# Three sums of weight quarters queued at the priority of their splits, and the scalar gates' columns moved behind the first mixer's projections

## The chip, the cores and the metric

The kernel runs on one core of a Trainium2 chip. The metric is the device time of one execution in microseconds (us), as a median of several runs. Five engines matter here: TensorE (PE in the profile; PEld is its weight load), VectorE (DVE), ScalarE (ACT), GpSimd (POOL) and SyncE (SP), which issues the transfers. Each works through its own list of instructions in the order in which they stand, and waits at the head of the list when an operand is not there.

## What is computed

A decoder trunk of two layers on 512 tokens of 1024 features, in float32:

```python
for i in range(DEPTH):                       # DEPTH = 2
    x = x + 0.5 * swiglu_ffn(rmsnorm(x, ffn1_norm[i]), ffn1_w_gu[i], ffn1_w_down[i])
    xn = rmsnorm(x, mix_norm[i])
    x = x + (ab_mixer(xn, ...) if i % 2 == 0 else nsa_mixer(xn, ...))
    x = x + 0.5 * swiglu_ffn(rmsnorm(x, ffn2_norm[i]), ffn2_w_gu[i], ffn2_w_down[i])
return rmsnorm(x, final_norm)
```

`swiglu_ffn` is `(silu(x @ w_gate) * (x @ w_up)) @ w_down` with 2816 hidden features. `ab_mixer` projects `xn` once into 512 channels of a gated linear recurrence (RG-LRU) and four mLSTM heads, whose scalar input and forget gates are eight columns of the projection. `nsa_mixer` is a sparse attention.

## The kernel before

**Products.** Every float32 operand is split in two: `hi`, its rounded part (ACT, a copy into float32r), and `lo`, the rest (DVE or POOL, `raw - hi`). A product of 128x128 weights is three matmuls, `hi*hi`, `hi*lo`, `lo*hi` (`mm3`, lines 177 to 179); the third is the first that needs the weights' `lo`. Weights stream from HBM: a transfer into a raw buffer (SP), the `hi` copy (ACT, line 171 or 320), the `lo` difference (line 172 or 321), then PE.

**The feed-forward blocks** (four, named f0a, f0b, f1a, f1b here). Of 22 slices of 128 hidden features the first four are multiplied directly; each of the other 18 is a pair (gate and up weights) that runs as seven products of half width after Strassen and Winograd, p1 to p7, each of twelve 256-column matmuls. They come in groups of 4, 8 and 6 slices; after each group the down projection of the group is added. `Pair.load` (line 301) brings a pair's four weight quarters (four transfers, lines 307 to 310, into two tiles `ra` and `rc`, both called `r` in the profile), forms three sums of them on DVE (lines 311 to 313; the first makes two sums at once) and splits the seven operands in four steps of `hi` (line 320) and `lo` (line 321): `ra[0:2]` for p1 and p7, `rc[0:2]` for p2 and p6, `ra[2:4]` for p5 and p4, and half as large `rc[2:3]` for p3. Two pairs of `r` tiles take turns, so that the transfers of a pair wait until the last splits of the pair two before have read their tile.

PE's order is written out by hand: p1, p7, then p3 of the pair before, p6, p2, p4, p5. The evictions of the products (lines 338 to 370) and what follows p3, the product of gate and up (line 372, DVE) and its `hi` and `lo` (line 390, ACT, and 391, DVE), are left to the scheduler like the sums and splits. The order of all engines but PE comes out of it: an instruction inside `tc.high_priority(offset=n)` is asked for n places earlier than it is written. The transfers and the sums have offset 400 (`RAHEAD`; 180, `RFIRST`, for the first two pairs of a block), the splits 230 (`SAHEAD`; 110, `SFIRST`), the evictions 320 (`EV`).

**The first mixer** (`ab`, line 479). Four turns of a loop each make four projections (24 matmuls of 512 columns each): channels of the recurrence (`rg_conv`), q, k (`qk`), and the output gate (`out_gate`). In the first turn the scalar gates' projection is made too, and `gate_rows` (line 569) works out from it on DVE and ACT the rows `G` and `EM` (names `misc` in the profile), by 12 DVE and 3 ACT steps. `gate_cols` (line 586) transposes them with eight small PE matmuls (lines 590 and 591) and copies the 128x32 result on DVE (line 592); the columns `gcol` are first read in the mLSTM loop. It stands at the end of the second turn. Behind the loop come `rg_gate(3)`, `rg_scan` (the recurrence, four channel groups of six DVE steps and one on ACT) and `proj_tok` (the v projection, lines 228 to 230), then the mLSTM loop over four chunks (lines 648 to 685).

A short chain of 128x4 steps (`sp`, lines 505 to 519: a transfer of `lam`, then one ACT exponential between some 25 DVE steps) prepares a constant of the recurrence. It is written at the head of `ab`, and the scheduler places it inside the last group of f0a, since nothing but `lam`, which takes the place of an `r` tile, holds it back.

Of the kernel before, what the change touches and what calls it, by code (L numbers as in the profile page):

```python
# [24 lines left out]
SAHEAD = 230  # L25
RAHEAD = 400
SFIRST = 110
# [29 lines left out]
def build(tc, a, out, stages=("f0a", "ab", "f0b", "f1a", "nsa", "f1b")):  # L57
    nc = tc.nc
    with ExitStack() as ctx:
# [16 lines left out]
        def blk(i, dt, name):  # L76
            return bp.tile([P, BW.get(i, 4 * T)], dt, name=name, tag=f"b{i}")
# [11 lines left out]
        def psum2():  # L89
            return pp.tile([P, T], F32, name="pt", bufs=8 - PSB)  # L90
# [205 lines left out]
        class Pair:  # L296
# [4 lines left out]
            def load(self, w, rb, first=False):  # L301
                with tc.high_priority(offset=RFIRST if first else RAHEAD):
                    ra, rc = (blk(rb[2 * (turns[1] % 2) + i], F32, f"r{i}")[:, :4 * T]
                              .rearrange("p (s c) -> p s c", s=4) for i in range(2))
                    turns[1] += 1

                    nc.sync.dma_start(ra[:, 0], w[0][:, :T])
                    nc.sync.dma_start(rc[:, 3], w[1][:, :T])
                    nc.sync.dma_start(ra[:, 3], w[1][:, T:])
                    nc.sync.dma_start(rc[:, 0], w[0][:, T:])  # L310
                    nc.vector.tensor_add(ra[:, 1:3], ra[:, 0:4:3], rc[:, 3:4].to_broadcast([P, 2, T]))  # L311
                    nc.vector.tensor_add(rc[:, 1], ra[:, 0], ra[:, 2])
                    nc.vector.tensor_add(rc[:, 2], rc[:, 0], rc[:, 1])
                with tc.high_priority(offset=SFIRST if first else SAHEAD):
                    for src, names in ((ra[:, 0:2], ("B11", "Q7")), (rc[:, 0:2], ("B21", "Q6")),
                                       (ra[:, 2:4], ("Q5", "Q4")), (rc[:, 2:3], ("B22",))):
                        hi, lo = parts()
                        m = len(names) * T
                        src = src.rearrange("p s c -> p (s c)")
                        nc.scalar.activation(hi[:, :m], src, AF.Copy)  # L320
                        nc.vector.tensor_sub(lo[:, :m], src, hi[:, :m].bitcast(F32))  # L321
                        for n, name in enumerate(names):
                            self.W[name] = hi[:, n * T:(n + 1) * T], lo[:, n * T:(n + 1) * T]
                return self
# [152 lines left out]
        def ab(x, nxt):  # L477
# [108 lines left out]
            def gate_cols():  # L586
                ps = psum2()
                for c in range(NT):
                    cs = slice(c * P, (c + 1) * P)
                    nc.tensor.transpose(ps[:, c * 8:c * 8 + 4], G[:, cs], ident[:4, :4])  # L590
                    nc.tensor.transpose(ps[:, c * 8 + 4:c * 8 + 8], EM[:, cs], ident[:4, :4])
                nc.vector.tensor_copy(gcol, ps[:, :NT * 8])
# [27 lines left out]
            for i in range(4):  # L620
                rg_conv(i)
                if i == 0:
                    gate_in()
                qk(i)
                qk(4 + i)
                if i == 0:
                    gate_rows()
                else:
                    rg_gate(i - 1)
                out_gate(i)  # L630
                if i == 1:
                    gate_cols()
            rg_gate(3)

            rg_scan()
            pss = proj_tok(a["ab_v"], x)
# [523 lines left out]
        first = [w[1:] for w in w0] if stages[0] == "f0a" else None  # L1160
# [129 lines left out]
```

## Time and profile before

| what | value |
|---|---|
| median of 3 runs | 2067.31 us (2062.09 to 2072.84) |
| the profiled execution, its own time | 2052.11 us |
| its span | 2050.4 us, 30519 instructions |
| PE busy | 1976.9 us, 96% of the span |
| DVE, ACT, POOL busy | 1372.1, 1027.8, 280.1 us |

The profiled execution is one run of its own; it is 15.2 us below the median of the three timed runs. Its rows are read for differences. In the rows a name such as `DVE L321 ... wx<-r,wx` is an engine, a line of the kernel and what is written from what; `wx` and `whi`, `wlo` are places of the splits, `ps` and `pt` are PSUM tiles. A time in brackets is how long the engine stood idle before the instruction, and what ended that. SPq marks an issue of a transfer.

### The profile page before, as it was taken

What the parts mean: (1) busy time and instruction counts of PE and PEld (TensorE: products, weight loads), DVE (VectorE), ACT (ScalarE), POOL (GpSimd) and SP (SyncE); (2) the same over time, 40 slices, a digit from 0 to 9 for tenths busy, and PEclk for the clock granted to TensorE, in tenths of its full rate; (3) what the DMA queues carried; (4) which work ended last, traced back from release to release, by engine and by line L of the source; (5) the groups of instructions that cost most, each with busy time, mean ns of one, the idle gap of its engine ahead of it and who ended that gap; (6) DMA issues with size and microseconds to landing.
All of it is one profiled execution on the core that took longest, in us unless ns stands there. A gap on an engine that the chain in (4) does not pass through costs nothing.

```text
span 2050.4 us, 30519 instructions
## 1 busy us (share of the span) xinstructions
PE 1976.9 (96%) x11896; PEld 1729.3 (84%) x11896; DVE 1372.1 (67%) x2189; ACT 1027.8 (50%) x1900; POOL 280.1 (14%) x290
## 2 busy tenths in 40 slices
PE   8899899989999998999999999999999999999997
PEld 6889899867788998897889989877777678999896
DVE  7847657489758657475966847443778788658474
ACT  5525436355545445254534525433888855446252
POOL 3000000343120000002000000201655540000002
PEclk9999999999999999999999999999999999999998
DMA  5232322322222323232232333321001032323212
GB/s 186 84 102 83 114 83 76 99 73 84 91 93 89 117 90 108 76 111 91 93 113 93 106 93 106 112 83 62 25 23 31 23 108 79 117 83 114 87 63 88
DMA packets 74737, 182.10 MB, mean 89 GB/s; under 512 B 8416, under 2 KB 9184, under 8 KB 74592
## 3 DMA queue, kind: packets, MB, share of 16 engines
q1 hardware_dynamic: 74448, 180.06, 28.2%
q8 instruction: 93, 1.52, 0.3%
q14 instruction: 52, 0.43, 0.1%
q10 hardware_dynamic: 144, 0.09, 0.0%
HBM read 178.02 MB, written 2.10 MB: 88 GB/s over the span
## 4 chain that ended last, share of the span: by engine, by line
PE 60%; DVE 9%; DMA 4%; issue 4%; ACT 2%; POOL 1%; SPq 0%; POOLq 0%; DVEq 0%; ACTq 0%
PE ps L177 14%; PE ps L178 14%; PE ps L179 14%; DMA r<-wgu 3%; PE pt L177 3%; PE pt L179 3%; PE pt L178 3%; PE px L999 2%; PE pt L789 2%; PE pt L1016 1%; DVE wlo L321 1%; PE pt L1017 1%; DVE wlo L172 1%; PE ps L955 1%; PE ps L958 1%
## 5 line engine op out<-in xcount | busy, mean ns | idle before, releaser
L171 ACT ACTIVATE whi<-raw 128x1024 fp32r<-128x1024 f32 (+2 forms) x196 | 193.3, 988 | 361.7 <-PE ps L178 250.8
L178 PE MATMUL ps<-h,whi 128*128 128x512 f32 x704 | 276.1, 392 | 1.1 <-DVE h L391 1.1
L179 PE MATMUL ps<-h,wlo 128*128 128x512 f32 x704 | 276.6, 393 | 0.0
L177 PE MATMUL ps<-h,whi 128*128 128x512 f32 x704 | 274.8, 391 | 1.3 <-ACT h L390 1.3
L320 ACT ACTIVATE whi<-r 128x1024 fp32r<-128x1024 f32 (+1 forms) x174 | 165.6, 952 | 194.4 <-PE ps L178 151.7
L172 DVE TENSOR_TENSOR wlo<-raw,whi 128x1024 fp32r<-128x1024 f32 (+2 forms) x166 | 192.7, 1164 | 73.1 <-ACT whi L171 68.0
L118 POOL TENSOR_TENSOR acc<-acc,t 128x512 f32<-128x512 f32 x48 | 75.5, 1573 | 1124.9 <-ACT t L116 1119.8
L458 DVE SCALAR_TENSOR_TENSOR X<-ps,X 128x512 f32<-128x512 f32 x96 | 66.3, 691 | 229.0 <-PE ps L179 229.0
L321 DVE TENSOR_TENSOR wlo<-r,whi 128x1024 fp32r<-128x1024 f32 (+1 forms) x174 | 188.6, 1086 | 24.1 <-ACT whi L320 23.8
L177 PE MATMUL ps<-x,whi 128*128 128x512 f32 x432 | 179.2, 415 | 0.5 <-ACT x L106 0.5
L179 PE MATMUL ps<-x,wlo 128*128 128x512 f32 x432 | 171.5, 397 | 0.0
L178 PE MATMUL ps<-x,whi 128*128 128x512 f32 x432 | 171.1, 396 | 0.3 <-DVE x L107 0.3
L311 DVE TENSOR_TENSOR r<-r,r 128x1024 f32<-128x1024 f32 x72 | 88.1, 1224 | 122.9 <-DMA r<-wgu 122.5
L178 PEld LDWEIGHTS ps<-h,whi 128*128 128x128 f32 x704 | 132.3, 188 | 31.9 <-DVE h L391 2.6
L177 PEld LDWEIGHTS ps<-h,whi 128*128 128x128 f32 x704 | 132.3, 188 | 30.5 <-ACT h L390 2.1
L179 PEld LDWEIGHTS ps<-h,wlo 128*128 128x128 f32 x704 | 132.4, 188 | 27.7
L177 PE MATMUL ps<-qB,whi 128*128 128x256 f32 x520 | 145.5, 280 | 2.5 <-ACT ps L364 2.4
L179 PE MATMUL ps<-qB,wlo 128*128 128x256 f32 x520 | 144.9, 279 | 0.6 <-DVE wlo L321 0.6
L178 PE MATMUL ps<-qB,whi 128*128 128x256 f32 x520 | 145.0, 279 | 0.0
L321 DVE TENSOR_TENSOR wx<-r,wx 128x1024 fp32r<-128x1024 f32 (+1 forms) x114 | 123.3, 1083 | 22.7 <-ACT wx L320 20.9
L390 ACT ACTIVATE h<-t 128x512 fp32r<-128x512 f32 x88 | 55.4, 630 | 139.0 <-DVE t L372 136.5
L320 ACT ACTIVATE wx<-r 128x1024 fp32r<-128x1024 f32 (+1 forms) x114 | 107.2, 941 | 6.2 <-DVE r L311 4.1
(340 smaller groups left out, 5442.4 us busy)
## 6 DMA issues: line engine op xcount, KB each, us to landing
r<-wgu SPq DMA_DIRECT2D x288, 256.0 KB, 3.6
raw<-wd SPq DMA_DIRECT2D x64, 512.0 KB, 3.5
raw<-wgu SPq DMA_DIRECT2D x30, 512.0 KB, 3.5
raw<-wd SPq DMA_DIRECT2D x32, 384.0 KB, 3.1
raw<-ab_fm SPq DMA_DIRECT2D x21, 512.0 KB, 3.5
raw<-nsa_fm SPq DMA_DIRECT2D x17, 512.0 KB, 3.5
raw<-ab_out SPq DMA_DIRECT2D x8, 512.0 KB, 3.5
raw<-nsa_out SPq DMA_DIRECT2D x16, 256.0 KB, 2.6
```

Source lines behind the costliest of these rows:

```text
L118: nc.gpsimd.tensor_add(acc, acc, sq)
L171: nc.scalar.activation(hi[:, :n], raw[:, :n], AF.Copy)
L172: (eng or nc.vector).tensor_sub(lo[:, :n], raw[:, :n], hi[:, :n].bitcast(F32))
L177: nc.tensor.matmul(ps, wh, xh, start=start, stop=False, skip_group_check=on)
L178: nc.tensor.matmul(ps, wh, xl, start=False, stop=False, skip_group_check=on)
L179: nc.tensor.matmul(ps, wl, xh, start=False, stop=stop, skip_group_check=on)
L311: nc.vector.tensor_add(ra[:, 1:3], ra[:, 0:4:3], rc[:, 3:4].to_broadcast([P, 2, T]))
L320: nc.scalar.activation(hi[:, :m], src, AF.Copy)
L321: nc.vector.tensor_sub(lo[:, :m], src, hi[:, :m].bitcast(F32))
L390: nc.scalar.activation(hh, t2, AF.Copy)
L458: nc.vector.scalar_tensor_tensor(X[i], ps, 0.5, X[i], op0=OP.mult, op1=OP.add)
L789: nc.tensor.matmul(p2[m][:, :155].rearrange("p (g n) -> p g n", g=5), w[:, q * 256 + m * P:q * 256 + (m + 1) * P], tt[:, :, n:n + 8 * 30 + ...
```

## The change

Two edits. The three sums in `Pair.load` leave the block of offset 400 and enter that of the splits (230, or 110); the four transfers stay. And `gate_cols()` leaves the second turn of the loop in `ab` and stands behind `rg_gate(3)`.

```diff
@@ -308,10 +308,10 @@
                     nc.sync.dma_start(rc[:, 3], w[1][:, :T])
                     nc.sync.dma_start(ra[:, 3], w[1][:, T:])
                     nc.sync.dma_start(rc[:, 0], w[0][:, T:])
+                with tc.high_priority(offset=SFIRST if first else SAHEAD):
                     nc.vector.tensor_add(ra[:, 1:3], ra[:, 0:4:3], rc[:, 3:4].to_broadcast([P, 2, T]))
                     nc.vector.tensor_add(rc[:, 1], ra[:, 0], ra[:, 2])
                     nc.vector.tensor_add(rc[:, 2], rc[:, 0], rc[:, 1])
-                with tc.high_priority(offset=SFIRST if first else SAHEAD):
                     for src, names in ((ra[:, 0:2], ("B11", "Q7")), (rc[:, 0:2], ("B21", "Q6")),
@@ -628,9 +628,8 @@
                 else:
                     rg_gate(i - 1)
                 out_gate(i)
-                if i == 1:
-                    gate_cols()
             rg_gate(3)
+            gate_cols()
 
             rg_scan()
```

The sums are lines 311 to 313 before and 312 to 314 in the changed kernel; the lines from `rg_gate(3)` on are one less. No instruction is added or removed on any engine. On DVE most sums stand one to five places later than before, behind splits (L321) and the steps of the pair before (L372, L391). On ACT some L390 stand earlier. On SP two pairs have two of their four transfers swapped, and nothing else moves. Of the 68 places where a pair follows another, the last sum goes from ahead of the earlier pair's last split (L321, 128x512) to behind it at 23.

DVE at the end of f0a's last group (r_3125 and r_3126 are the tiles of its last pair, wx_3134 and wx_3137 the `lo` for its p1 and p6, spw the chain for `sp`), before:

```order
L321 TENSOR_TENSOR wlo<-r_3002,whi 128x512
L321 TENSOR_TENSOR wx_3137<-r_3126,wx_3137 128x1024
L372 TENSOR_TENSOR t_2918<-t_2903,t_2918 128x512
L321 TENSOR_TENSOR wx_3134<-r_3125,wx_3134 128x1024
L391 TENSOR_TENSOR h_430<-t_2918,h_430 128x512
L506 SCALAR_TENSOR_TENSOR spw_3535<-misc 128x4
L321 TENSOR_TENSOR wlo<-r_3125,whi 128x1024
```

and now:

```order
L321 TENSOR_TENSOR wlo<-r_3002,whi 128x512
L365 TENSOR_TENSOR t_2918<-ps,t_2918 128x256
L314 TENSOR_TENSOR r_3126<-r_3126 128x512
L506 SCALAR_TENSOR_TENSOR spw_3535<-misc 128x4
L321 TENSOR_TENSOR wx_3137<-r_3126,wx_3137 128x1024
L508 TENSOR_SCALAR spw_3536<-spw_3535 128x4
...
L372 TENSOR_TENSOR t_2918<-t_2903,t_2918 128x512
...
L359 TENSOR_TENSOR t_3042<-pt,t_3042 128x256
L321 TENSOR_TENSOR wx_3134<-r_3125,wx_3134 128x1024
```

The chain for `sp` has moved in front of wx_3134: L506 (which reads `lam`), L508 (which waits for ACT's exponential, L507) and nine more 128x4 steps stand before L372, five more between it and L359.

DVE in the group of eight of f1a, at its last but one pair (r_10450, r_10451; r_10848 is the next one's), before:

```order
L365 TENSOR_TENSOR t_10243<-ps,t_10243 128x256
L321 TENSOR_TENSOR wlo<-r_10327,whi 128x512
L321 TENSOR_TENSOR wx_10462<-r_10451,wx_10462 128x1024
L372 TENSOR_TENSOR t_10243<-t_10228,t_10243 128x512
L321 TENSOR_TENSOR wx_10459<-r_10450,wx_10459 128x1024
L391 TENSOR_TENSOR h_9036<-t_10243,h_9036 128x512
L311 TENSOR_TENSOR r_10848<-r_10848,r_10849 128x1024
```

and now:

```order
L321 TENSOR_TENSOR wlo<-r_10327,whi 128x512
L365 TENSOR_TENSOR t_10243<-ps,t_10243 128x256
L314 TENSOR_TENSOR r_10451<-r_10451 128x512
L312 TENSOR_TENSOR r_10848<-r_10848,r_10849 128x1024
L321 TENSOR_TENSOR wx_10462<-r_10451,wx_10462 128x1024
L321 TENSOR_TENSOR wx_10459<-r_10450,wx_10459 128x1024
L372 TENSOR_TENSOR t_10243<-t_10228,t_10243 128x512
```

The first sum of the next pair, which waits for that pair's transfers, has moved in front of both first splits of this pair. At four more places (r_1632, r_6858, r_11326, r_17274) it has moved from between the two to in front of both, and at one (r_9202) to in front of one; at eight it has moved behind both.

PE at the end of the second turn of `ab`'s loop (x_3292 to x_3295 are the mixer's input), before:

```order
L177 MATMUL ps<-x_3293,whi 128x512
L178 MATMUL ps<-x_3295,whi 128x512
L179 MATMUL ps<-x_3293,wlo 128x512
L590 MATMUL pt<-ident,misc 128x4
L591 MATMUL pt<-ident,misc 128x4
```

and now:

```order
L177 MATMUL ps<-x_3293,whi 128x512
L178 MATMUL ps<-x_3295,whi 128x512
L179 MATMUL ps<-x_3293,wlo 128x512
L177 MATMUL ps<-x_3292,whi 128x512
L178 MATMUL ps<-x_3294,whi 128x512
L179 MATMUL ps<-x_3292,wlo 128x512
```

The third turn's `rg_conv` follows `out_gate(1)` directly; the eight transposes stand behind L540 of `rg_gate(3)` and ahead of L228. On DVE the copy L592 has moved from the second turn to a place among the first steps of `rg_scan`, and nothing else of `ab` has moved there or on ACT and POOL.

## Rows read from the trace of the kernel before

**Rows 1.** The page: busy time of each engine, share of the span, instructions.

```profile
PE 1976.9 (96%) x11896; PEld 1729.3 (84%) x11896; DVE 1372.1 (67%) x2189; ACT 1027.8 (50%) x1900; POOL 280.1 (14%) x290
```

**Rows 2.** Windows: length; PE, PEld, DVE, ACT, POOL busy; PEclk; DMA share; GB/s. Strassen stretches.

```profile
59.39:107.96 48.57, 42.45 (x336) 41.71 (x335) 41.06 (x52) 27.39 (x47) 0.00 (x0) 0.93 0.34 100
...
sum 746.34, PE 718.25 PEld 711.82 DVE 580.77 ACT 438.60 POOL 1.37; mean PE 59.85 PEld 59.32 DVE 48.40 ACT 36.55 POOL 0.11
```

**Rows 3.** Waits: who waited for whom, total us, times, longest us.

```profile
DVE r L311 <- DMA r<-wgu: 122.5, 60, 6.6
...
PE ps L177 <- ACT ps L364: 8.2, 8, 2.8
```

**Rows 4.** Timeline (start us, duration us, instruction, idle time before it), end of f0a's eight.

```profile
230.58 1.23 DVE L311 TENSOR_TENSOR r<-r,r 128x1024 f32<-128x1024 f32 x1 [3.97 <-DMA r<-wgu]
231.72 0.68 DVE L372 TENSOR_TENSOR t<-t,t 128x512 f32<-128x512 f32 x1
232.32 0.68 DVE L312 TENSOR_TENSOR r<-r 128x512 f32<-128x512 f32 x1
232.44 0.63 ACT L390 ACTIVATE h<-t 128x512 fp32r<-128x512 f32 x1 [4.36 <-DVE t L372]
...
233.39 0.58 PE L177 MATMUL ps<-qQ,whi 128*128 128x256 f32 x1 [3.96 <-ACT t L354]
```

**Rows 5.** Window of the matmuls behind that stall.

```profile
232.95:236.37 3.42, 2.98 (x14) 2.98 (x15) 3.42 (x5) 1.61 (x4) 0.00 (x0) 0.50 0.01 2
```

**Rows 6.** Timeline, one of the shorter waits of PE.

```profile
1171.26 0.39 PE L177 MATMUL ps<-qB,whi 128*128 128x256 f32 x1 [1.48 <-ACT ps L364]
```

**Rows 7.** Timeline, f0a's last group, SP, ACT, PE, DVE; landing of `lam` after its issue.

```profile
326.80 0.33 SPq L505 DMA_DIRECT2D misc<-lam  x1
...
DMA to landing us min/median/max: 1.5/1.5/1.5
...
330.37 1.28 ACT L507 ACT_TABLE_LOAD   x1
331.67 0.21 ACT L507 ACTIVATE spw<-spw 128x4 f32<-128x4 f32 x1
...
331.80 0.28 PE L179 MATMUL ps<-qB,wx 128*128 128x256 f32 x1
...
333.93 0.16 DVE L514 TENSOR_TENSOR spw<-spw,spw 128x4 f32<-128x4 f32 x1
334.13 0.17 DVE L515 TENSOR_SCALAR spw<-spw 128x4 f32<-128x4 f32 x1
```

**Rows 8.** Timeline, f1a's group of eight, SP, DVE and PE.

```profile
1155.10 0.33 SPq L308 DMA_DIRECT2D r<-wgu  x1
...
1158.71 1.23 DVE L311 TENSOR_TENSOR r<-r,r 128x1024 f32<-128x1024 f32 x1 [0.20 <-DMA r<-wgu]
...
1160.09 0.28 PE L179 MATMUL ps<-qB,wx 128*128 128x256 f32 x1
```

**Rows 9.** Timeline, PE at the gates' transposes; DVE's split for the projection behind them.

```profile
428.88 0.39 PE L179 MATMUL ps<-x,wlo 128*128 128x512 f32 x1
431.52 0.19 PE L590 MATMUL pt<-ident,misc 4*128 4x4 f32 x1 [2.25 <-DVE misc L581]
436.78 0.26 PE L591 MATMUL pt<-ident,misc 4*128 4x4 f32 x1 [5.07 <-ACT misc L584]
...
431.46 2.12 DVE L172 TENSOR_TENSOR wlo<-raw,whi 128x1024 fp32r<-128x1024 f32 x1
```

**Rows 10.** Windows: the half-speed stretch there; from `rg_scan` to the mLSTM loop.

```profile
434.34:441.17 6.83, 4.39 (x15) 3.63 (x16) 4.10 (x8) 3.58 (x5) 0.96 (x1) 0.50 0.46 157
481.83:517.43 35.60, 35.11 (x167) 27.90 (x165) 35.49 (x32) 19.47 (x25) 11.86 (x6) 1.00 0.26 83
```

**Rows 11.** Timeline, DVE before `rg_scan`, and PE's first wait in the mLSTM loop.

```profile
479.78 0.69 DVE L523 TENSOR_TENSOR t<-ps,R 128x512 f32<-128x512 f32 x1 [1.12 <-PE ps L179]
...
518.32 0.46 PE L650 MATMUL ps<-qT,kT 128*128 128x128 f32 x2 [1.38 <-DVE mlast L655]
```

## The prediction

> **What bounds the kernel now.** I read five views, from the coarse to the fine.
>
> The page comes first. PE is busy for 1976.9 of 2050.4 us, DVE for 67% [rows 1]. No change that moves instructions can take off much more than the 73.5 us in which PE stands idle, or shorten matmuls that run at half clock. So the question is which idle times of PE the two edits reach.
>
> The windows over the twelve Strassen stretches follow: they last 746.34 us, PE is busy in 718.25 of them, and 28.1 us are idle [rows 2]. The first stretch holds 6.1 of these (48.57 less 42.45); there the evictions wait for the block's activations, which no edit touches.
>
> The list of waits says who is late. DVE stands 60 times, 122.5 us in all, in front of a first sum (L311) whose transfers have not landed [rows 3]. Yet PE waits only eight times for an eviction of ACT (L364), 8.2 us in all: DVE's waiting mostly stays hidden. The timeline shows how it comes out where it doesn't [rows 4]. A first sum waits 3.97 us; behind it stands L372, which depends on no transfer; behind L372 on ACT stand L390 and the evictions, and PE waits 3.96 us. The next 3.42 us run at half clock: 14 matmuls, where the first stretch's rate (42.45 us for 336) gives 1.77 us, so that 1.65 us more are lost [rows 2, 5]. There are two such long stalls, 3.96 and, as the longest behind L364, 2.8 us [rows 3, 4]. In both the order of DVE is the same in the changed kernel (the first sum has not passed L372), so I leave them. The rest is 28.1 - 6.1 - 3.96 - 2.8 = 15.2 us in short waits like the one at 1171.26 [rows 2, 3, 4, 6].
>
> Last, the mixer: PE stands 2.25 and 5.07 us before the gates' transposes, 7.3 us [rows 9]. Behind them it works at half clock up to 441.17; of the 4.4 us from 436.78 on, half, 2.2 us, is lost [rows 9, 10]. That is 9.5 us in one place, the largest that the change touches.
>
> **The gates' columns.** The wait goes from this place, but what comes out at the end is another matter. `rg_conv(2)`'s projection now follows the matmul at 428.88. The first stretch makes a matmul of 256 columns every 0.126 us [rows 2], so I estimate 0.25 us for these of 512. Its third needs the `lo` of L172, and that step runs on DVE from 431.46 for 2.12 us, up to 433.58, behind the gates' rows, which have not moved [rows 9]. So PE stands from 428.88 + 3 x 0.25 = 429.6 to 433.6: a new wait of 4.0 us, as long as the one that ended in half clock at 233.39 [rows 4, 5]. PE leaves it some 4 us ahead of today.
>
> Can the lead be kept? From 481.83 to 517.43 DVE is busy for 35.49 of 35.60 us, and PE then waits 1.38 us for DVE's `mlast` [rows 10, 11]. DVE's work there is unchanged, one copy (L592) having moved into it. So the end of that stretch moves only as far as DVE can start earlier, and DVE's one wait for PE ahead of it is 1.12 us, at 479.78 [rows 11]. Of 4 us, at most 1.1 come through. The copy of 128x32 costs between a 128x4 step, 0.20 us from start to start [rows 7], and a 128x512 one, 0.60 [rows 4]; nearer the second with its handover, so I take 0.5 and **-0.6** in all, with -1.1 as one end. The other end: if the transposes, behind `rg_gate(3)`, hold up the v projection behind them, or if DVE is delayed by the copy's wait for them, the half-clock stretch (1.65 us) and one handover of 3 us like the stalls' add up to +5.
>
> By the row at 232.95 PE works at half clock behind a wait of 4 us [rows 4, 5]. The Trainium skill's page TensorE: Matmul & The Clock Gate, section "HAM oscillation — how this bites in real kernels", says that each idle gap of some length makes the matmuls behind it start at half rate, and that this is paid again at each gap. By that page alone, taking the gates' wait away would give its half-speed matmuls back as well, 2.2 us on top; the trace speaks against counting them, since the new 4.0 us wait is of the kind that is followed by half clock.
>
> **The sums, the usual pair.** No sum costs more; what changes is who goes first on DVE. Of 68 successions the earlier pair's last split now precedes the later pair's last sum at 23. That split frees the `r` tile and feeds p3; ahead of it one 128x512 step less stands, 0.60 us from start to start [rows 4]. Where a short wait of PE hangs on that order it shrinks by 0.60. I have not traced each of the 18 short waits to its order, so I take the same share of them: 18 x 23/68 = 6, 6 x 0.60 = -3.6. The wait at 1171.26 (1.48) goes whole: L372, on which its eviction waits, now stands ahead of the first sum [rows 6]. Together **-5.1**. The ends: 0, since an earlier split only lets a transfer be asked for earlier and DVE may wait for it all the same; -15.2, all the short waits.
>
> **The chain of `sp`.** L505, the transfer of `lam`, goes out when a last split frees its place, now at 326.80 [rows 7]. One L372, one last sum and one 128x256 step (0.60 + 0.60 + 0.30, by [rows 4]) no longer stand ahead of that split: 325.3. It lands 1.5 later, at 326.8 [rows 7]. Then L506 waits for it on DVE with wx_3134 behind it, the split that p1's third matmul needs at 331.80. ACT's table load, which needs no data and covers L506, and the exponential take 1.28 + 0.21: 328.3 [rows 7]; the split wx_3137, 1.14, runs in their shade. Nine steps at 0.20, L372 at 0.60, five more steps, one of 0.30, and wx_3134 at 1.14: 328.3 + 1.8 + 0.6 + 1.0 + 0.3 + 1.1 = 333.1 [rows 4, 7]. PE ran the third matmul at 331.80, so **+1.3**; ends 0 (the evictions elsewhere give the slack) and +3.0 (the landing is no earlier than today: +1.5 more).
>
> **The first sum put ahead of splits.** At r_10848 the first sum now stands ahead of both splits of the pair in front. The tile's transfers go out 1.5 us earlier by the same three steps, L308 at 1153.6 instead of 1155.10, so the landing that ended DVE's wait at 1158.71 comes at 1157.2 [rows 8]. Then 1.14 for the sum, 1.14 and 1.23 for the two splits give 1160.7, against PE's third matmul at 1160.09 [rows 4, 8]: **+0.6**; ends 0 and +2.3 (landing unmoved: 1.5 later, and a handover). Four more places have the sum ahead of both where it stood between the two; there only one split is behind it that was not, and I take 0, with +0.5 each as an end. The eight places where it moved back give nothing that I count, since the sum waited there.
>
> **Sum.** -0.6 - 5.1 + 1.3 + 0.6 = **-3.8 us**. The terms are read from the profiled execution, which lasted 2052.11 us, 1.7 more than its span and 15.2 less than the median of 2067.31. I take the difference as the same at the median: **2063.5 us**. About 0.5%, 10.3 us, is what a measurement of this kernel can tell from no change. With the ends of all terms this case runs from about 2056 to 2074, and I widen it by a microsecond or so for the median itself.
>
> **Rivals.**
>
> *Slower: first sums hold back splits.* DVE is strictly in order in these rows: L372 stood 3.97 us behind a sum that waited for a DMA [rows 4]. At five places and in the chain of `sp`, six in all, a step that waits for a transfer now precedes a split that PE needs. The price at each is the split's 1.14 us, which PE waits, and 1.65 us of half clock behind it: 6 x 2.8 = 17; less the gains of 3.8, about +13, so **2080**. It decides where the first sum (or L506) starts less than 1.14 us earlier than now. For it: landings are DVE's main wait [rows 3]. Against: what is asked for earlier lands earlier, and PE stood only 8.2 us in all behind 122.5 us of such waits.
>
> *The gates' whole wait comes off.* If DVE's solid stretch isn't the bound, because its head start grows with PE's, 9.5 instead of 0.6 comes off: -3.8 - 8.9 = -12.7, **2054.6**. For it: 9.5 us is the largest idle place here. Against: DVE at 35.49 of 35.60 [rows 10].
>
> *All short waits go.* If each of the 18 hangs on sums that precede what PE waits for, -15.2 replaces -5.1 and the two losses vanish: -15.8, **2051.5**. For it: the releaser of most is an eviction behind L372. Against: only a third of the orders change.
>
> *Sums no later in effect.* If DVE waits at the same landings whatever precedes them, the result is within 1 us of 2067; that lies inside my forecast.
>
> **How the numbers follow.** My forecast, with the last case, has 0.70; slower 0.12; gates 0.10; short waits 0.08. The range of **2053 to 2075** takes in the forecast and the gates' case and leaves out the other two, 0.20. Faster by over 0.5% (below 2057) are the gates' and the short waits' cases and 0.04 of the forecast's: 0.22; slower (above 2077.6) is its rival, 0.12; the same 0.66.
>
> **What would show it.** Right: a wait of about 4 us at some 429.6 with half clock behind it, no transposes there, and PE still waiting for `mlast` at about 517.5; the wait at 1171 gone; a wait of some 1.3 us near 331.8; the two long stalls as they were. Wrong: DVE's stretch before the mLSTM loop begins several us earlier (gates); new waits of PE for L321 wx at p1's third matmul in several pairs (slower); Strassen stretches with far less than 22 us idle (short waits).

## The result, and the profile after

| | before | changed |
|---|---|---|
| median | 2066.49 us (4 runs, 2062.09 to 2072.84) | 2044.47 us (4 runs, 2039.48 to 2048.05) |
| profiled execution, its own time | 2052.11 us | 2039.48 us |
| span | 2050.4 us | 2037.7 us |

The changed kernel is faster by 22.0 us: ratio 0.9895, 95% interval 0.9872 to 0.9917. The forecast was 2063.5 us, with a range of 2053 to 2075; the result lies below it. The two profiled executions differ by 12.7 us only. One execution can lie 10 us from the median (the profiled one of sums_only below took 2050.32 us, where its median was 2040.95), so times are compared by medians, and traces are read for patterns that several of them show.

The page, busy times of the changed kernel:

```profile
PE 1974.5 (97%) x11896; PEld 1727.6 (85%) x11896; DVE 1370.5 (67%) x2189; ACT 1031.3 (51%) x1900; POOL 282.7 (14%) x290
```

The work is the same [rows 1]; what went is mostly idle time of PE, 63.2 us in place of 73.5. The windows over its Strassen stretches, the first and the sum of the twelve:

```profile
58.87:106.78 47.91, 42.22 (x337) 41.40 (x336) 41.09 (x51) 27.45 (x47) 0.00 (x0) 0.93 0.34 107
...
sum 736.61, PE 715.78 PEld 711.20 DVE 580.14 ACT 442.18 POOL 3.75; mean PE 59.65 PEld 59.27 DVE 48.34 ACT 36.85 POOL 0.31
```

736.61 us in place of 746.34 [rows 2], 9.7 of the 12.7 us. Second traces (after_again and before_again, below) give 731.84 us in place of 748.58. The changed kernel's waits:

```profile
DVE r L312 <- DMA r<-wgu: 109.1, 50, 6.3
ACT h L390 <- DVE t L372: 94.7, 56, 4.8
...
PE ps L179 <- DVE wx L321: 6.8, 8, 1.9
...
PE ps L177 <- ACT ps L364: 5.8, 5, 1.9
```

First sums wait for transfers 109.1 us in place of 122.5, and PE 5.8 us for L364 in place of 8.2 [rows 3]. In this trace the place that the forecast left alone, the end of f0a's group of eight, changes too:

```profile
227.11 1.22 DVE L312 TENSOR_TENSOR r<-r,r 128x1024 f32<-128x1024 f32 x1 [2.78 <-DMA r<-wgu]
228.25 0.68 DVE L372 TENSOR_TENSOR t<-t,t 128x512 f32<-128x512 f32 x1
...
228.97 0.63 ACT L390 ACTIVATE h<-t 128x512 fp32r<-128x512 f32 x1 [1.65 <-DVE t L372]
...
229.92 0.38 PE L177 MATMUL ps<-qQ,whi 128*128 128x256 f32 x1 [1.25 <-ACT t L354]
```

The chain of rows 4 stands in the same order as before, first sum, L372, L390, eviction, PE, but PE waits 1.25 us in place of 3.96 [rows 4]. That is no gain of the change. Ten microseconds earlier PE had stood 1.90 us at 220.18, where it stood 1.12 us before, and then it worked at half clock (granted clock 0.50 from 221.24 to 224.65). So its work between the two waits took 8.49 us in place of 6.97, and it came to the second one later. In the second trace of the changed kernel, without such a wait at 220, the stall is back:

```profile
230.27 0.58 PE L177 MATMUL ps<-qQ,whi 128*128 128x256 f32 x1 [3.71 <-ACT t L354]
```

The second trace of the kernel before has 3.70 us there. The long stall at the end of f0b's group of eight did shrink, and does so in both traces of the changed kernel (2.82 and 2.54 us before, 1.57 and 1.46 now). Before, and changed:

```profile
816.73 0.58 PE L177 MATMUL ps<-qB,wx 128*128 128x256 f32 x1 [2.82 <-ACT ps L364]
```

```profile
809.17 0.39 PE L177 MATMUL ps<-qB,wx 128*128 128x256 f32 x1 [1.57 <-ACT ps L364]
```

Where the order at a stall did not change, but its length did in several traces, I read the stall as inherited from what came before it.

The first sums of f0b's group of eight show the inheritance. Timeline of DVE, the kernel before:

```profile
746.77 1.22 DVE L311 TENSOR_TENSOR r<-r,r 128x1024 f32<-128x1024 f32 x1 [3.25 <-DMA r<-wgu]
758.62 1.23 DVE L311 TENSOR_TENSOR r<-r,r 128x1024 f32<-128x1024 f32 x1 [1.73 <-DMA r<-wgu]
770.16 1.23 DVE L311 TENSOR_TENSOR r<-r,r 128x1024 f32<-128x1024 f32 x1 [3.23 <-DMA r<-wgu]
781.64 1.23 DVE L311 TENSOR_TENSOR r<-r,r 128x1024 f32<-128x1024 f32 x1 [3.17 <-DMA r<-wgu]
791.15 1.23 DVE L311 TENSOR_TENSOR r<-r,r 128x1024 f32<-128x1024 f32 x1 [0.44 <-DMA r<-wgu]
801.68 1.23 DVE L311 TENSOR_TENSOR r<-r,r 128x1024 f32<-128x1024 f32 x1 [2.22 <-DMA r<-wgu]
812.70 1.22 DVE L311 TENSOR_TENSOR r<-r,r 128x1024 f32<-128x1024 f32 x1 [2.72 <-DMA r<-wgu]
```

The changed kernel:

```profile
742.09 1.22 DVE L312 TENSOR_TENSOR r<-r,r 128x1024 f32<-128x1024 f32 x1 [3.47 <-DMA r<-wgu]
754.19 1.23 DVE L312 TENSOR_TENSOR r<-r,r 128x1024 f32<-128x1024 f32 x1 [2.20 <-DMA r<-wgu]
764.64 1.23 DVE L312 TENSOR_TENSOR r<-r,r 128x1024 f32<-128x1024 f32 x1 [1.55 <-DMA r<-wgu]
774.55 1.22 DVE L312 TENSOR_TENSOR r<-r,r 128x1024 f32<-128x1024 f32 x1 [3.35 <-DMA r<-wgu]
785.84 1.23 DVE L312 TENSOR_TENSOR r<-r,r 128x1024 f32<-128x1024 f32 x1
794.68 1.23 DVE L312 TENSOR_TENSOR r<-r,r 128x1024 f32<-128x1024 f32 x1 [1.72 <-DMA r<-wgu]
805.04 1.22 DVE L312 TENSOR_TENSOR r<-r,r 128x1024 f32<-128x1024 f32 x1 [2.06 <-DMA r<-wgu]
```

From the first row to the last it is 65.93 us before and 62.95 now (65.70 and 62.58 in the second traces): the series has gained 3 us over six pairs, and the PE stall behind the last row is what shrinks. Nearly every first sum waits for its transfers in both series. This can be read as a loop: first sum, splits, tile free, transfer, and the first sum two pairs on. The experiments test it.

The other steps, on the timeline and in windows of the changed kernel: the gates' place, and `mlast`;

```profile
427.95 2.12 DVE L172 TENSOR_TENSOR wlo<-raw,whi 128x1024 fp32r<-128x1024 f32 x1
...
430.12 0.79 PE L179 MATMUL ps<-x,wlo 128*128 128x512 f32 x1 [3.96 <-DVE wlo L172]
...
513.01 0.77 PE L649 MATMUL ps<-qT,kT 128*128 128x128 f32 x2 [2.11 <-DVE mlast L654]
```

```profile
429.45:436.28 6.83, 6.16 (x15) 4.81 (x16) 5.08 (x7) 2.20 (x3) 0.00 (x0) 0.50 0.45 156
...
476.10:512.00 35.90, 34.80 (x170) 27.51 (x168) 35.80 (x33) 19.45 (x25) 11.57 (x6) 0.99 0.27 88
```

and p1's third matmul of f0a's last pair, which had no wait before [rows 7]:

```profile
328.35 0.39 PE L179 MATMUL ps<-qB,wx 128*128 128x256 f32 x1 [0.84 <-DVE wx L321]
```

### The profile page after: what moved, and what is told of

It is laid out like the page before. It is cut to its first block, busy times and chain, and to the rows that moved or that the text cites. A ratio compares the mean times of both kernels' runs of the same rounds, so it can differ in the third digit from the quotient of the medians.

```text
span 2037.7 us, 30533 instructions
## 1 busy us (share of the span) xinstructions
PE 1974.5 (97%) x11896; PEld 1727.6 (85%) x11896; DVE 1370.5 (67%) x2189; ACT 1031.3 (51%) x1900; POOL 282.7 (14%) x290
## 4 chain that ended last, share of the span: by engine, by line
PE 59%; DVE 10%; issue 4%; DMA 3%; ACT 2%; POOL 1%; POOLq 0%; DVEq 0%; SPq 0%; ACTq 0%
PE ps L179 14%; PE ps L178 14%; PE ps L177 14%; DMA r<-wgu 3%; PE pt L179 3%; PE pt L177 3%; PE pt L178 3%; PE px L998 2%; PE pt L788 2%; DVE wx L321 1%; PE pt L1015 1%; DVE wlo L172 1%; PE pt L1016 1%; PE ps L954 1%; PE ps L957 1%
## 5 line engine op out<-in xcount | busy, mean ns | idle before, releaser
L172 DVE TENSOR_TENSOR wlo<-raw,whi 128x1024 fp32r<-128x1024 f32 (+2 forms) x166 | 192.8, 1165 | 72.2 <-ACT whi L171 67.3
L321 DVE TENSOR_TENSOR wlo<-r,whi 128x1024 fp32r<-128x1024 f32 (+1 forms) x174 | 188.7, 1087 | 27.4 <-ACT whi L320 27.1
L312 DVE TENSOR_TENSOR r<-r,r 128x1024 f32<-128x1024 f32 x72 | 88.0, 1224 | 111.6 <-DMA r<-wgu 109.1
L321 DVE TENSOR_TENSOR wx<-r,wx 128x1024 fp32r<-128x1024 f32 (+1 forms) x114 | 122.8, 1082 | 19.9 <-ACT wx L320 16.9
L390 ACT ACTIVATE h<-t 128x512 fp32r<-128x512 f32 x88 | 55.5, 630 | 97.9 <-DVE t L372 94.7
```

The costliest lines, as they stand in the source:

```text
L172: (eng or nc.vector).tensor_sub(lo[:, :n], raw[:, :n], hi[:, :n].bitcast(F32))
L390: nc.scalar.activation(hh, t2, AF.Copy)
```

## The experiments

Each was run against the kernel before on the same chip. Unless said otherwise an edit is made to the kernel before. A control comes first.

**before_again and after_again**: both kernels once more.

> The kernel before once more, unchanged, so that its times and its trace are seen on the chip that runs the next three. Expected ratio 1.000. The profiled execution seen so far took 2052.11 us, the timed runs 2062 to 2073, and the changed kernel gained 12.6 us by the profiles but 22 us by the medians. Theory V (the first profiled execution was a lucky one): this trace has a span of 2060 to 2070 us and 9 or 10 us more in a few long waits and half-speed stretches than the first trace (which had six stretches at half clock). Theory W (the runs are alike, the difference lies outside the span): a span near 2050 us with a time near 2066 us.

> The changed kernel once more, unchanged, on the chip that runs the next three, so that they stand beside it. Expected ratio 0.988 to 0.992 as measured first (0.9895). If the two parts add up (0.9993 and 0.9915 of the first batch), 0.9908.

Measured: 1.0011 (0.9999 to 1.0022), 2060.09 us beside 2057.05, a span of 2055.2 us; and 0.9894 (0.9873 to 0.9915), 2038.05 us. The change's effect repeats. Theory V is right in part: this trace of before is 4.8 us longer than the first, and has nine half-speed stretches in place of seven (the end of the program counted), but the medians of the kernel before also differ by up to 10 us between the first comparison (2066) and the later ones (2057 to 2060).

**gates_only and sums_only**: one part of the change each.

```diff
gates_only
-                if i == 1:
-                    gate_cols()
             rg_gate(3)
+            gate_cols()
sums_only
+                with tc.high_priority(offset=SFIRST if first else SAHEAD):
                     nc.vector.tensor_add(ra[:, 1:3], ra[:, 0:4:3], rc[:, 3:4].to_broadcast([P, 2, T]))
                     nc.vector.tensor_add(rc[:, 1], ra[:, 0], ra[:, 2])
                     nc.vector.tensor_add(rc[:, 2], rc[:, 0], rc[:, 1])
-                with tc.high_priority(offset=SFIRST if first else SAHEAD):
```

> Only the gates' columns are moved; the sums stay as before. Theory G (the mixer's end is set by DVE): -1 to -3 us, ratio 0.9985 to 0.9995, with a wait of 4 us for L172 at about 430 us and the mLSTM loop starting 1 to 2 us earlier, as the trace of the full change has it (-3.5 us before the place, -5.2 us behind it). Theory H (the whole wait comes off): -9 us, ratio 0.9955.

> Only the three sums are moved; the gates' columns stay in the second turn. Theory G: the sums carry nearly all, -19 to -21 us, ratio 0.990 to 0.991. Theory H: -12 to -13 us, ratio 0.994. Either way the waits of ACT's L390 for L372 fall from 136.5 us to about 95 us, and PE's waits for L364 from 8.2 us to 4 us or less.

Measured: gates 0.9993 (0.9977 to 1.0009), about -1.4 us, not clear of no change; sums 0.9915 (0.9897 to 0.9932), about -17.5 us. Theory G holds, H falls. PE's waits in gates_only, timeline:

```profile
436.31 0.53 PE L179 MATMUL ps<-x,wlo 128*128 128x512 f32 x1 [4.00 <-DVE wlo L172]
...
519.17 0.77 PE L649 MATMUL ps<-qT,kT 128*128 128x128 f32 x2 [3.33 <-DVE mlast L654]
```

The new wait for L172 is there, and what PE keeps of its lead it loses waiting for `mlast`, 3.33 us in place of 1.38 [rows 11].

**first_only and later_only**: which of the three sums.

```diff
later_only: the first sum keeps RAHEAD
                     nc.vector.tensor_add(ra[:, 1:3], ra[:, 0:4:3], rc[:, 3:4].to_broadcast([P, 2, T]))
+                with tc.high_priority(offset=SFIRST if first else SAHEAD):
                     nc.vector.tensor_add(rc[:, 1], ra[:, 0], ra[:, 2])
                     nc.vector.tensor_add(rc[:, 2], rc[:, 0], rc[:, 1])
first_only: the first sum alone goes into SAHEAD
+                with tc.high_priority(offset=SFIRST if first else SAHEAD):
                     nc.vector.tensor_add(ra[:, 1:3], ra[:, 0:4:3], rc[:, 3:4].to_broadcast([P, 2, T]))
+                with tc.high_priority(offset=RFIRST if first else RAHEAD):
                     nc.vector.tensor_add(rc[:, 1], ra[:, 0], ra[:, 2])
                     nc.vector.tensor_add(rc[:, 2], rc[:, 0], rc[:, 1])
```

> Only the second and third sum are moved to the splits' offset; the first sum, the one that waits for the transfers, keeps offset 400; the gates' columns stay. Theory S (the gain is the last split's: one short sum less ahead of it, so the tile is free earlier): nearly the gain of sums_only, -10 to -20 us. Theory F (the gain is the first sum's: L372 goes ahead of it and no longer waits for a landing): 0 to -4 us, ratio 0.998 to 1.000, and ACT's waits for L372 near 136 us as before.

> Only the first sum is moved to the splits' offset; the second and third keep offset 400 (they can still not stand ahead of the first, whose result they read); the gates' columns stay. Theory F (the gain is that L372 of the pair before no longer stands behind a first sum that waits for its transfers; it passes the first sum at the same 16 places as in the full change and at four more): -12 to -18 us, ratio 0.991 to 0.994, and ACT's waits for L372 near 95 us. Theory S (the gain needs the last split ahead of the last sum): 0 to -4 us, ratio 0.998 to 1.000.

Measured: later_only 0.9983 (0.9966 to 1.0000), -3.5 us, with an interval that reaches no change; first_only 0.9915 (0.9894 to 0.9937), -17.5 us, all that the three sums give together. It is the first sum, the one that waits for transfers. Theory F, that L372 is freed from standing behind it, was the next to be tried.

**mulonly_320 and sums_at16**: L372 past the first sum without moving the sums, and the sums moved only where L372 passes.

```diff
mulonly_320
-                with tc.high_priority(offset=EV // 2):
+                with tc.high_priority(offset=320):
                     nc.vector.tensor_mul(self.t2, self.t1, self.t2)
+                with tc.high_priority(offset=EV // 2):
                     self.down(self.t2)
sums_at16 (sums_rest: not in)
+                late = turns[1] - 1 in (7, 9, 17, 21, 27, 29, 33, 34, 43, 44, 47, 49, 52, 59, 62, 64)
+                with tc.high_priority(offset=(SFIRST if first else SAHEAD) if late else (RFIRST if first else RAHEAD)):
```

> The sums stay at offset 400 and the gates' columns in the second turn, as before; only L372, the product of gate and up, is asked for earlier, at offset 320 in place of 160. It passes the first sum at nine of the 16 places of the full change and at five others, and no split passes a first sum. Theory F: -6 to -12 us, ratio 0.994 to 0.997, and ACT's waits for L372 down from some 136 us by a third. Theory S (it is the splits' places and the tiles they free): 0 to +4 us, since the splits stand no earlier than before, some even behind a second sum.

> The three sums are moved at 16 of the 72 pairs only, those at which the full change lets L372 of an earlier pair pass the first sum (13 of the 16 still do so here); at the other 56 pairs the sums keep offset 400; the gates' columns stay. Theory F16 (the gain sits at these crossings): -12 to -17 us, ratio 0.992 to 0.994, and ACT's waits for L372 near 95 us. Rival R56 (the gain comes from many small steps everywhere, the splits and evictions that pass the later sums): 16/72 of 17.5 us, so -4 us, ratio 0.998.

> The complement: the three sums are moved at the other 56 pairs and keep offset 400 at the 16; none of the 16 crossings happens (four others do); the gates' columns stay. Theory F16: 0 to -5 us, ratio 0.9975 to 1.000. Rival R56: -12 to -14 us, ratio 0.993 to 0.994.

Measured: mulonly_320 1.0008 (0.9993 to 1.0023); sums_at16 0.9993 (0.9977 to 1.0009); sums_rest 0.9927 (0.9905 to 0.9950), -15 us. Theory F, as what carries the gain, falls three times over. In mulonly_320 first sums do wait less than in before, but PE's waits have a new name:

```profile
DVE r L311 <- DMA r<-wgu: 114.6, 60, 6.4
...
PE ps L179 <- DVE wlo L321: 4.2, 4, 1.9
```

In the kernel before, that last wait was 0.6 us, once.

**before_noload and after_noload**: no transfers in the loop. Behind the first two pairs of each feed-forward block, the r tiles keep their quarters and are used again; the products with the other weights are left out.

```diff
+                    if len(kept) < 2:
+                        kept.append([...])
                         ra, rc = kept[-1]
                         nc.sync.dma_start(ra[:, 0], w[0][:, :T])
...
+                    ra, rc = kept[turns[1] % 2]
```

> The kernel before, but in each feed-forward block only the first two pairs have their quarters transferred; the other pairs use the two sets of r tiles again (so the products of the other weights are left out, and all engines but SP have the same instructions). No first sum waits for a transfer any more behind the first two pairs. Theory L (the stretches are held back by a loop: a first sum waits for its transfers, its splits follow on DVE, the last of them frees the tile, and only then the transfers of the pair two further on are asked for; the sums' move shortens this loop): the idle time in the Strassen stretches falls from about 40 us of excess to under 20 us, -18 to -28 us, ratio 0.986 to 0.991. Theory O (the order of sums, splits and products on DVE costs PE time by itself): -5 us or less, ratio over 0.9975.

> The same with the changed kernel. Theory L: without the loop the sums' move has nothing left to shorten: the distance to the kernel before without transfers is that of the gates' columns alone, 0 to -4 us (so a ratio of 0.984 to 0.991). Theory O: the sums' move still brings its 15 to 18 us here, a distance of -16 to -22 us between the two.

Measured: 0.9825 (0.9801 to 0.9849), 2022.51 us, and 0.9815 (0.9792 to 0.9837), 2022.21 us. Without transfers the two kernels are 0.3 us apart by their medians. This prices the sums' move less well than it seems to: in the order that came out, the first sums stand in the same place among the splits at 69 of the 72 pairs of the two kernels, so that the move is hardly there. What the runs do show is that the idle time hangs on the transfers. In before_noload first sums stand ahead of 115 more splits, counted over all pairs, than in the kernel before, and yet PE's idle time there is 7.4 us, 6.3 of it in the first stretch: the order by itself costs next to nothing, and theory O falls. Theory L fits, but so does any account in which a first sum that waits for its transfers keeps other work of DVE waiting. The transfers do not slow DVE's steps themselves (a first sum takes 1.22 us on average with them and without, a split 1.08 and 1.09). The windows over the Strassen stretches, before_noload, with its second stretch, and then the sum for after_noload:

```profile
152.13:229.88 77.75, 77.75 (x672) 77.75 (x671) 65.15 (x84) 49.23 (x86) 0.00 (x0) 1.00 0.01 2
...
sum 716.28, PE 708.90 PEld 707.68 DVE 592.42 ACT 446.87 POOL 1.56; mean PE 59.07 PEld 58.97 DVE 49.37 ACT 37.24 POOL 0.13
```

```profile
sum 714.79, PE 708.47 PEld 707.16 DVE 592.58 ACT 446.90 POOL 1.56; mean PE 59.04 PEld 58.93 DVE 49.38 ACT 37.24 POOL 0.13
```

The group of eight has no idle time left, and 30.1 us of the 746.34 are gone. By this measure the transfers cost the kernel before some 36 us in all, and the sums' move took off about half as much.

**before_spare and after_spare**: the loop shortened in another way; the third sum is rounded, so that its `lo` is left out.

```diff
-                    nc.vector.tensor_add(rc[:, 2], rc[:, 0], rc[:, 1])
+                    last = spare[0] if spare else rc[:, 2]
+                    nc.vector.tensor_add(last, rc[:, 0], rc[:, 1])
...
+                spare[:] = [lo[:, T:2 * T]]
```

> The kernel before, but the third sum is written to the unused half of the lo slot of the pair before (rounded to float32r there, so that its lo part is left out) and the last split reads it from there. The tile rc is then free after its second split, and its two transfers go out before those of ra, one to two us earlier; ra still waits for the third split. Theory L: the loop is 1 us or so shorter in every turn, -6 to -15 us, ratio 0.993 to 0.997. Theory O: no gain or a loss, since first sums now stand ahead of one more split: 0 to +5 us.

> The same with the changed kernel. Theory L: it gains less than on the kernel before, as the loop there is already shorter: 0 to -6 us against the changed kernel, ratio 0.986 to 0.990. Theory O: 0 to +5 us against the changed kernel, 0.990 to 0.992.

Measured: 0.9947 (0.9927 to 0.9966), -11 us on the kernel before, as theory L has it; but 0.9954 (0.9939 to 0.9969) with the change, 12 us slower than the changed kernel itself, which neither theory had. In its order first sums stand ahead of 58 more splits (at 43 pairs) and ahead of 25 more L372 than in the changed kernel: the scheduler placed them earlier, at the same offset, and so undid the move. The two spare kernels have nearly the same order (first sums differ in their place among the splits at 6 of 72 pairs), and their times are not told apart. PE's longest waits in after_spare are those of rows 4, for the eviction behind L372 (here L357, L354 before), 12.1 us in place of 6.1 in the kernel before:

```profile
PE ps L177 <- ACT t L357: 12.1, 6, 3.8
```

**first_at8 and first_at4**: the first sum moved at a few of the 56 pairs.

```diff
+                late = turns[1] - 1 in (3, 8, 20, 23, 28, 53, 57, 63)
+                with tc.high_priority(offset=(SFIRST if first else SAHEAD) if late else (RFIRST if first else RAHEAD)):
                     nc.vector.tensor_add(ra[:, 1:3], ra[:, 0:4:3], rc[:, 3:4].to_broadcast([P, 2, T]))
```

> Only the first sum, and only at eight of the 72 pairs (the 4th, 9th, 21st, 24th, 29th, 54th, 58th and 64th loaded), is moved to the splits' offset; all else is as before. At each of these one split of the pair in front (and nothing else of the splits) passes the first sum, as in sums_rest; L372 passes at four of them. Theory P (the loop is longest where a split still stands behind a first sum that waits for its transfers; these eight carry what sums_rest gave): -9 to -15 us, ratio 0.993 to 0.9955. Rival Q (the gain is spread over all the sums' places): 8/72 of 17 us, -2 us, ratio 0.999.

> The same at four of the eight pairs only (the 9th, 29th, 54th and 64th), those whose first sum waited 1.9 to 3.3 us in the trace of before; the first sums of the other four of the eight waited 0 to 0.5 us. Theory P: nearly all of first_at8's gain, -7 to -13 us, ratio 0.994 to 0.9965. If the waiting does not matter: half of it, -5 to -7 us. Rival Q: -1 us, ratio 0.9995.

Measured: 0.9982 (0.9971 to 0.9993) and 0.9982 (0.9968 to 0.9996), -3.7 us each. Theory P falls: eight places don't carry it. Rival Q, a gain spread over all the places (ratios of 0.999 and 0.9995), lies inside both intervals and stands. sums_at16 and sums_rest, which share out the pairs, add up: 1.4 and 15 us, to the 17.5 of all. But in sums_rest the first sum passes splits and L372 at the same places as in first_at8, and adding the 3.5 us of the later sums to first_at8's 3.7 gives only half of its 15, a gap little larger than the intervals. Which of the 72 places matter is not settled.

**first_gates, lam_own and first_gates_lam**: towards a faster version, the last two with a tile of its own for `lam` (lam_own on the changed kernel).

```diff
-            lam = misc[:, 516 + 3 * T:520 + 3 * T]
+            lam = cp.tile([P, 4], F32, name="lam")
```

> The changed kernel with the second and third sum back at offset 400: only the first sum and the gates' columns are moved. If the first sum carries all that the sums give (0.9915 alone, as the three sums together) and the gates add what they added so far: ratio 0.9895, the same as the full change. If its four further crossings of L372 count: -2 to -4 us more, 0.9875 to 0.9885.

> The changed kernel with a tile of its own for lam in place of a part of the r tile that it had, so that its transfer no longer waits for that tile's last split; the scheduler places it, the exponential and the 25 small DVE steps at the start of the program. The forecast's step on the chain of sp says that the wait of 0.8 to 1.1 us for L321 at p1's third matmul of f0a's last pair (near 328 us) goes: -1 to -2 us against the changed kernel, ratio about 0.989. If the 25 steps and the table load cost as much at the new place: no difference from the changed kernel.

> The same with a tile of its own for lam. On the changed kernel this tile brought no difference that was clear of noise (0.9912 beside 0.9894). Expected the same as first_gates, within 0.002 in the ratio; lower by 0.0005 to 0.001 if the wait at p1's third matmul of f0a's last pair counts.

Measured: 0.9906 (0.9884 to 0.9929), 0.9912 (0.9889 to 0.9934), 0.9919 (0.9901 to 0.9938). None is clear of the changed kernel's 0.9894; no faster version was found.

**The loop's length, from the traces.** For 28 first sums (the last five of each group of eight, counting the next group's first, and the last two of each group of six, in four blocks) I took from each trace the time from the first sum two pairs ahead to this one, and cut it at the issue of L308, which waits for the last split:

```
us, mean of 28         one turn   first sum to L308   L308 to first sum   waits of all first sums   ratio
before (two traces)  22.31 22.52    18.51 18.63         3.80 3.89             122.5 121.7            1.0011
gates_only              22.48          18.62               3.85                125.0                 0.9993
sums_at16               22.33          18.36               3.97                127.5                 0.9993
first_at8               22.34          18.37               3.97                120.1                 0.9982
first_at4               22.32          18.30               4.02                120.6                 0.9982
later_only              22.03          18.31               3.72                117.3                 0.9983
mulonly_320             21.98          18.20               3.79                114.6                 1.0008
sums_rest               21.97          18.02               3.95                112.6                 0.9927
first_only              21.75          17.72               4.03                 96.6                 0.9915
sums_only               21.52          17.68               3.84                110.1                 0.9915
changed (two traces) 21.73 21.30    17.72 17.52         4.01 3.78             109.1 100.1            0.9894
before_spare            20.74            -                   -                 128.6                 0.9947
after_spare             21.04            -                   -                 134.4                 0.9954
```

(The fourth column is DVE's waiting for transfers in front of all 72 first sums. In the spare kernels the transfers of one tile go out ahead of the other's, so the cut at L308 does not compare.)

PE needs 2 x 84 matmuls for two pairs, 168 x 77.75/672 = 19.4 us without idle time (before_noload's second stretch). All turns are longer, so PE loses its lead pair by pair and stands at the group's end: in the four groups of eight of the first trace of before, PE's waits come to 0.3, 0.9, 3.6 and 10.6 us in the first to the last quarter of a group. The time from L308 to the first sum is much the same throughout; what the first sum's move shortens is the part from the first sum to the last split, by 0.9 us or so. Two loops run side by side, so 28 turns are the length of 14: 14 x 0.9 = 13 us for these alone, as much as the Strassen stretches of the traces lost (746.34 and 748.58 us before, 736.61 and 731.84 in the changed kernel) and most of the 17.5. The rest is not assigned.

How the move comes to PE is argued, not shown. Without the spare kernels the ratios rank by the turn, but for mulonly_320, whose splits are late (its waits above); they rank about as well by the fourth column, the time in which a waiting first sum holds up what stands behind it on DVE. And the spare kernels speak against the turn alone: theirs is shorter than the changed kernel's, and they are slower than it, with first sums that wait longest of all. So two ways stay open side by side: tiles that come free earlier, and ready work (splits, L372) that no longer stands behind a waiting first sum. No run separates them.

## Why the forecast was wrong

**The step that failed is "The sums, the usual pair", -5.1 us.** Its direction was right, but it looked at the wrong sum and mis-sized the term by a factor of three (-17.5 by sums_only). It priced the last sum behind the last split, 0.60 us at six of 18 short waits. The runs showed the first sum in its place: alone it gave all of the 17.5 us (first_only), the later sums alone 3.5, hardly clear of no change (later_only). Moved behind splits and L372, first sums wait 96.6 us for transfers in place of 122.5, the loop turns 0.6 to 0.8 us faster (first_only), and in the two traces of the changed kernel PE's idle time in the Strassen stretches is 20.8 and 15.9 us, in place of 28.1 and 29.2. The row for it had been read, 122.5 us [rows 3]. The forecast took it as hidden, since PE waited 8.2 us only for the evictions behind it, and so had no term for it. By which way the first sum's place comes to PE stays open, as said above; that it needs the transfers is shown.

Two readings of the forecast were off, with little weight in its sum. In the first stretch it is PE itself that stands, 5.6 of the 6.1 us for the quarters `qQ` of the activations, and not the evictions; and of the 18 waits of PE outside that stretch two are the long ones, so that 16 are short and the term would have been 0.4 us smaller.

The decision "In both the order of DVE is the same in the changed kernel (the first sum has not passed L372), so I leave them" was right for one of the two long stalls: f0a's is 3.71 us in after_again, 3.89 in first_only and 3.60 in sums_only, and only in the first trace 1.25. It was wrong for f0b's, 1.57 and 1.46 us in place of 2.82 and 2.54 (1.54 in first_only, though 3.04 in sums_only): a microsecond or so came off there with the order unchanged.

**The gates: right.** -0.6 was forecast, -1.4 measured, not clear of no change. The wait of 4.0 us for L172 came as 3.96, PE worked at half clock behind it (0.50 from 429.45 to 436.28), and `rg_scan`'s stretch is as full of DVE as before, 35.80 of 35.90 us. The half-speed matmuls were not given back, as the trace of before had spoken for: before the change the granted clock was 0.50 from 434.34 to 441.17 [rows 10]. The Trainium skill, page TensorE: Matmul & The Clock Gate, section "HAM oscillation — how this bites in real kernels", has the cost of a cold start paid again at each such gap; the trace agrees.

**The chain of `sp`: right in place and nearly in size.** +1.3 was forecast for p1's third matmul near 331.8; the wait is there with 0.84 us (1.10 in sums_only, 1.11 in after_again), from no wait. It is not worth more in the end: lam_own, where the chain stands at the start of the program, was no faster.

**The first sum ahead of splits: right in place and nearly in size.** L308's row for this pair and the sum stand as forecast, 1.7 us or so earlier against PE. The third matmul that ran at 1160.09 without a wait [rows 8] is now at 1150.53, and it waits for its split 0.38 us where +0.6 was forecast (0.39 in after_again, 0.25 in sums_only):

```profile
1150.53 0.38 PE L179 MATMUL ps<-qB,wx 128*128 128x256 f32 x1 [0.38 <-DVE wx L321]
```

The wait at 1171.26 went whole, as forecast: its matmul, now at 1160.37, has none to speak of.

**The rivals.** "First sums hold back splits" (2080) did not come true here; its mechanism exists: the 0.38 us above are a case of it, and in after_spare, where first sums were put back ahead of splits and L372, 12 us were lost although the loop's turn is shorter. "The gates' whole wait" (2054.6) is excluded by gates_only. "All short waits go" (2051.5) was nearest in time, and it was partly what happened: counted as the forecast counts them, the short waits come to 12.3 and 5.1 us in the two traces of the changed kernel, in place of 15.2 and 17.3. They shrink, but they don't go, and the gain went beyond its 15.8 us.

**The range.** Its lower end came from adding up short waits. With 122.5 us of first sums that wait, and a turn of 22.3 us where PE needs 19.4, the bound to look at was what the transfers cost: up to 36 us could go, as the kernels without transfers show.

## What to carry to other kernels

When an engine waits for a transfer again and again, and the transfer waits for a tile that this engine frees, measure the turn of that loop and compare it with the bounding engine's time for the same pieces: if it is longer, the waits are not hidden, though the bounding engine shows few of its own. They can add up over a stretch and come out as a stall near its end. But a shorter turn is no promise of a shorter time (before_spare, after_spare): on an engine that works in order, an instruction that waits for a transfer should also stand late, so that ready work does not stand behind it. Before a stall in one trace is explained, look for it in a second trace of the same kernel: the one that shrank most here was back in the next.

## What was not expected of the hardware

The spread between executions: executions of one kernel on one chip differ by 10 us and more (2032.9 to 2050.3 for sums_only), and the medians of the kernel before by nearly 10 between comparisons (2066, then 2057 to 2060). TensorE's granted clock goes with it: of sums_only's executions the longest had 0.985 over the whole, the shortest 0.991. One profiled execution of each kernel is not enough to size a change of 1%.
